# Twelve pairs of a dense expert lookup get their first product early, in a two-block transformer kernel

## The chip, the cores and the metric

The kernel runs on one core of one Trainium2 chip. The metric is the device time of one execution in microseconds; the median of three timed runs is 4170.13 (4164.8 to 4174.73).

## The reference, cut to what matters

Two transformer blocks on 256 tokens of width 1024 in float32. The first block ends in a mixture of 32 experts with two weight matrices in (gate, up) and one out (down), four experts per token. The second block has two streams, context and latent (256 tokens each) and two layers; the context stream goes through the first layer only. Each layer ends in a lookup:

```python
q = (xb @ w_q).reshape(PEER_BLOCK, PEER_HEADS, 2, PEER_HALF)
s = einsum('thpd,pkd->thpk', q, sub_keys)
s1, i1 = top_k(s[:, :, 0], 16)
s2, i2 = top_k(s[:, :, 1], 16)
cand_s = s1[..., :, None] + s2[..., None, :]
cand_i = i1[..., :, None] * 128 + i2[..., None, :]
top_s, pos = top_k(cand_s.reshape(128, 8, 256), 16)
idx = take_along_axis(cand_i.reshape(128, 8, 256), pos)
wts = softmax(top_s)
act = gelu(einsum('thkd,td->thk', u_tab[idx], xb)) * wts
out = einsum('thk,thkd->td', act, v_tab[idx])
```

There are 16384 rows in u_tab and in v_tab. Three such lookups are computed: the context's, the latent's in layer 0, the latent's in layer 1.

## The kernel before, in words

The lookup is computed densely: for all 16384 rows the product with every token, times a grid of gates that is zero where a token did not choose the row. It has two parts.

`peer_prep` (line 808) makes the grid. It multiplies by `w_q` (line 156 to 158), scores the keys (line 723), ranks them on VectorE with `top16` (lines 701 to 709), and reads out the chosen expert numbers (line 760): for each of 8 heads and 16 choices one operation that compares a ramp with the position and sums the candidates' numbers where it matches. That is done for two halves of 128 tokens each. Then `grid` multiplies one-hot matrices (lines 792 to 803) and sends the grid to memory.

`peer_pass` (line 830) goes over 64 pairs of 256 rows each. A pair's first product (`u_stage`, lines 156 to 158, 48 matmuls of 256 columns) needs two weight tiles of 128x1024 from `p_u`. `wload` splits each into a high half (line 146, ScalarE) and a low half (line 147, VectorE), and the product is made of three matmuls, high by high, high by low, low by high. Then come gelu (line 873), the gates (line 894), a split of the result (lines 117, 118), and the second product with two tiles of `p_v` (lines 906 to 909, 24 matmuls of 512 columns), which add up in four PSUM banks over all pairs. Weight tiles rotate over three buffers each of raw, high and low. The latent lookups make 40 and 48 of their pairs' first products ahead of the loop (`early`); those kept in memory are written to `sdr` and read back by `prefetch`.

The experts (`moe`, line 962) run two at a time: gate and up products for two halves of 512 columns (line 1088, each half closed by a bias product, line 1091), a hidden layer, transposes (line 1110), the down product (line 1122) and the sum into tokens (line 1134). Each expert pair needs 24 weight tiles of 1 MB (tile `mo`, four buffers, issued by SyncE).

The order on each engine is made by a scheduler from priorities: the experts come first, and code under `filler` (the context stream and its lookup) fills in. After the first two expert pairs `overflow` (line 1138) tests whether any expert has more than 64 tokens; the test is a branch that every engine takes (line 1143), and the code behind it is issued after it, apart from what the scheduler placed ahead. Of the context lookup's `peer_prep` eight steps are ahead of the test. The last two pairs' loads wait for the last expert load (`late`).

The lines of the change as they are numbered after it stand up to 26 higher: the split is 147 and 148, the test 1155, gate and up 1100, the bias product 1103, down 1134.

Of the kernel before, what the change touches and what calls it, by code (L numbers as in the profile page):

```python
# [10 lines left out]
F32 = mybir.dt.float32  # L11
# [9 lines left out]
P = 128  # L21
# [17 lines left out]
B_LATE = 2  # L39
MT = "u"  # L40
# [4 lines left out]
PF = 2  # L45
# [19 lines left out]
def kernel(ctx: ExitStack, tc: tile.TileContext, a: dict, out: bass.AP):  # L65
# [74 lines left out]
    def wload(src, n=1024, get=load, s=None):  # L140
        wr = wraw(s)
        get(wr[:, :n], src)
        pl, nb = s or (st, WB)
        wh = pl.tile([P, 1024], F32R, tag="wh", name="wh", bufs=nb[1])
        wl = pl.tile([P, 1024], F32R, tag="wl", name="wl", bufs=nb[1])
        nc.scalar.activation(wh[:, :n], wr[:, :n], AF.Copy)  # L146
        low = nc.vector.tensor_sub(wl[:, :n], wr[:, :n], wh[:, :n].bitcast(F32))  # L147
        if hold[1]:
            queued(low, hold[0])
            hold[1] -= 1  # L150
        return wh, wl
# [559 lines left out]
    def topk(l, q, tk, idx, pt):  # L711
        keys, qT = q
        sc = []
        for tb in range(2):
# [42 lines left out]
            for h in range(8):  # L757
                for k in range(16):
                    eq = eqs[:, k % 8, 0:NCAND]
                    nc.vector.scalar_tensor_tensor(eq, iota[:, 0:NCAND], tf[:, h, k:k + 1], ce[:, h, :], op0=ALU.is_equal,  # L760
                                                   op1=ALU.mult, accum_out=ef[:, h, k:k + 1])
                if h % 2:
                    yield
# [66 lines left out]
    def peer_pass(l, xm, pp, gd, consume, ahead=None, after=None, late=None, mark=None, npair=64, wide_end=False):  # L830
# [14 lines left out]
        def fetch(dst, src):  # L845
            ins = nc.sync.dma_start(dst, src)
            queued(ins, after[0] if after else None)
            if late is not None and at_pair[0] >= npair - late[0]:
                queued(ins, late[1])
            if mark is not None:  # L850
                mark[:] = [ins.ins]

        def u_stage(pr, nat):
            bank = psum("u")
            for c in range(2):
# [5 lines left out]
                else:  # L861
                    wh, wl = wload(a["p_u"][l, 2 * pr + c], get=load if pr in rank else fetch)
# [72 lines left out]
        for pr in early:  # L935
# [3 lines left out]
            yield "ahead"  # L939
        grid_fetch(0)  # L940
        prev = None
        for pr in range(npair):
            at_pair[0] = pr
            prefetch(pr + PF)
# [12 lines left out]
        yield npair  # L957

# [263 lines left out]
    with filler():  # L1222
# [31 lines left out]
        bprep = peer_prep(0, XB, tkb, gds[0], (2, NB1, 3), "u")  # L1254
# [4 lines left out]
    with filler():  # L1259
        general("u", "a")  # L1260
        drain(bprep)
        tkb_stack.close()
        pp_stack = ctx.enter_context(ExitStack())
        pp = pool("pp", stack=pp_stack, side="right")
        bpass = peer_pass(0, XB, pp, gds[0], late_res(bres, cdr, 0, 1, 5, pp, "gr"), late=(B_LATE, mres["last"]), mark=bmark)
# [415 lines left out]
```

## Time and profile before

| | us |
|---|---|
| median of three runs | 4170.13 |
| profiled execution | 4162.7 |
| its span | 4160.9 |
| TensorE busy | 4013.7 (96%) |
| VectorE busy | 2382.3 (57%) |
| ScalarE busy | 1929.2 (46%) |
| GpSimd busy | 168.9 (4%) |
| mean granted clock of TensorE | 0.983 |

The page gives the busy time of each engine over the whole span; a view by stages gives it for any stretch, with the granted clock of TensorE and the share of time in which the 16 DMA engines moved data. A timeline gives the start of single instructions and, in brackets, how long the engine sat idle ahead of one and what released it. PE is TensorE, PEld its weight loads, DVE VectorE, ACT ScalarE, POOL GpSimd, SP SyncE; a q behind the name is the engine's sequencer.

### The profile page before, as it was taken

To read this page: it belongs to the slowest core of one execution; us is meant where nothing else is said; L and a number is where in the kernel's file an instruction comes from. 1 tells how busy PE (TensorE), PEld (TensorE's weight loads), DVE (VectorE), ACT (ScalarE), POOL (GpSimd) and SP (SyncE) were. 2 spreads that over 40 slices of the span, in tenths; PEclk is the share of its full clock that TensorE was granted. 3 is DMA by queue.
4 is the path that set the end of the run, shared out by engine and by line. 5 is a ranking of instruction groups with operands and counts; after the bars stand their busy time and mean duration, and the time that the engine had idled before them with its cause. 6 is when DMAs were issued, how large, how long until landed. Compare 5 with 4: busy or idle time off the path is not lost. (4 is left out here: it accounts for less than half of the span.)

```text
span 4160.9 us, 63155 instructions
## 1 busy us (share of the span) xinstructions
PE 4013.7 (96%) x23786; PEld 3064.1 (74%) x23786; DVE 2382.3 (57%) x6357; ACT 1929.2 (46%) x2836; POOL 168.9 (4%) x230
## 2 busy tenths in 40 slices
PE   8999979999999999999998999999998899999998
PEld 7686535566666666666578999788777699988887
DVE  4465686543333333333278997565455789766555
ACT  5543245533333333333243886345545349744443
POOL 0000001100000000000000120000000002200000
PEclk9999989999999999999999999999998899999999
DMA  7659878998889898998865578776774246787773
GB/s 254 240 180 359 338 268 335 348 335 327 338 325 339 322 348 320 338 340 331 319 208 169 205 257 320 258 238 218 261 255 153 98 154 231 260 294 242 235 236 127
DMA packets 340046, 1115.47 MB, mean 268 GB/s; under 512 B 28935, under 2 KB 128007, under 8 KB 283673
## 3 DMA queue, kind: packets, MB, share of 16 engines
q1 hardware_dynamic: 323896, 1043.22, 69.9%
q10 hardware_dynamic: 15552, 66.07, 4.0%
q8 instruction: 189, 3.10, 0.3%
q0 software_dynamic: 288, 2.10, 0.1%
q14 instruction: 121, 0.98, 0.1%
HBM read 1041.97 MB, written 69.30 MB: 267 GB/s over the span
## 5 line engine op out<-in xcount | busy, mean ns | idle before, releaser
L147 DVE TENSOR_TENSOR wl<-wr,wh 128x1024 fp32r<-128x1024 f32 x933 | 1132.1, 1221 | 1045.2 <-ACT wh L146 1038.3
L146 ACT ACTIVATE wh<-wr 128x1024 fp32r<-128x1024 f32 x933 | 980.0, 1055 | 1264.0 <-PE ps_u L157 521.4
L907 PE MATMUL ps_a<-wl,ah 128*128 128x512 f32 x1536 | 587.2, 398 | 2.9 <-DVE wl L147 2.8
L906 PE MATMUL ps_a<-wh,ah 128*128 128x512 f32 x1536 | 572.0, 397 | 0.1
L1088 PE MATMUL ps_g<-mo,xg 128*64 128x512 f32 x2048 | 472.9, 605 | 15.5 <-DMA mo<-in_w_up_dram 11.3
L909 PE MATMUL ps_a<-wh,al 128*128 128x512 f32 x1536 | 478.3, 396 | 0.0
L906 PEld LDWEIGHTS ps_a<-wh,ah 128*128 128x128 f32 x1536 | 288.0, 188 | 79.4 <-issue 12.5
L907 PEld LDWEIGHTS ps_a<-wl,ah 128*128 128x128 f32 x1536 | 286.3, 188 | 76.0 <-issue 13.3
L909 PEld LDWEIGHTS ps_a<-wh,al 128*128 128x128 f32 x1536 | 286.8, 188 | 71.3 <-issue 6.1
L1088 PEld LDWEIGHTS ps_g<-mo,xg 128*64 128x64 f32 x2048 | 137.8, 138 | 269.5 <-issue 236.9
L156 PE MATMUL ps_u<-xbh,wh 128*128 128x256 f32 x1088 | 313.3, 288 | 1.6 <-ACT ge L873 1.6
L157 PE MATMUL ps_u<-xbl,wh 128*128 128x256 f32 x1088 | 312.7, 288 | 0.0
L158 PE MATMUL ps_u<-xbh,wl 128*128 128x256 f32 x1088 | 312.6, 287 | 0.0
L156 PE MATMUL ps_u<-xah,wh 128*128 128x256 f32 x960 | 276.0, 288 | 2.9 <-ACT sp L873 2.7
L158 PE MATMUL ps_u<-xch,wl 128*128 128x256 f32 x960 | 274.1, 287 | 4.1 <-DVE wl L147 4.1
L158 PE MATMUL ps_u<-xah,wl 128*128 128x256 f32 x960 | 273.8, 287 | 2.4 <-DVE wl L147 2.4
L157 PE MATMUL ps_u<-xal,wh 128*128 128x256 f32 x960 | 275.5, 287 | 0.0
L157 PE MATMUL ps_u<-xcl,wh 128*128 128x256 f32 x960 | 274.6, 286 | 0.0
L156 PE MATMUL ps_u<-xch,wh 128*128 128x256 f32 x960 | 274.5, 286 | 0.0
L802 DVE TENSOR_SCALAR o<-cst,it 128x128 f32<-128x128 f32 x768 | 233.2, 347 | 38.8 <-PE ps_a L803 38.3
L1122 PE MATMUL ps_g<-mo,hT 128*64 128x512 f32 x1024 | 239.8, 611 | 8.5 <-DMA mo<-in_w_down_dram 5.3
L803 PE MATMUL ps_a<-o,o 128*128 128x128 f32 x1536 | 227.6, 278 | 11.8 <-ACT o L798 9.4
(652 smaller groups left out, 7004.8 us busy)
## 6 DMA issues: line engine op xcount, KB each, us to landing
wr<-in_p_u_dram SPq DMA_DIRECT2D x384, 512.0 KB, 4.7
wr<-in_p_v_dram SPq DMA_DIRECT2D x384, 512.0 KB, 4.9
mo<-in_w_gate_dram SPq DMA_DIRECT2D x128, 1024.0 KB, 8.5
mo<-in_w_up_dram SPq DMA_DIRECT2D x128, 1024.0 KB, 7.4
mo<-in_w_down_dram SPq DMA_DIRECT2D x128, 1024.0 KB, 8.2
gd<-stg ACTq DMA_DIRECT2D x48, 1024.0 KB, 6.5
gr<-gd SPq DMA_DIRECT2D x96, 512.0 KB, 7.7
mw<-in_w_mod_dram SPq DMA_DIRECT2D x48, 512.0 KB, 5.3
```

Of the source, the lines that this page charges most:

```text
L146: nc.scalar.activation(wh[:, :n], wr[:, :n], AF.Copy)
L147: low = nc.vector.tensor_sub(wl[:, :n], wr[:, :n], wh[:, :n].bitcast(F32))
L156: nc.tensor.matmul(o, wh, xh, start=first, stop=False)
L157: nc.tensor.matmul(o, wh, xl, start=False, stop=False)
L158: nc.tensor.matmul(o, wl, xh, start=False, stop=last)
L802: nc.vector.tensor_scalar(o1, iota, it[:, 0, t:t + 1], it[:, 2, t:t + 1], op0=ALU.is_equal, op1=ALU.mult)
L803: nc.tensor.matmul(bank[:, 2 * i2 + i, :], o2q[:, i, :], o1, start=True, stop=True)
L906: nc.tensor.matmul(acc[tb][hf], ah[:, ts], wh[:, hs], start=first, stop=False)
L907: nc.tensor.matmul(acc[tb][hf], ah[:, ts], wl[:, hs], start=False, stop=False)
L909: nc.tensor.matmul(acc[tb][hf], al[:, ts], wh[:, hf * 512:(hf + 1) * 512], start=False, stop=fin)
L1088: nc.tensor.matmul(bank[64 * i:64 * i + 64, :], xg[:, kq * 4 + k, o:o + CAP], wt[i][:, k, :], start=(kq == 0 and k == 0), stop=False, skip ...
L1122: nc.tensor.matmul(bank[64 * i:64 * i + 64, :], hT[:, kq * 4 + k, 64 * i:64 * i + 64], wt[i][:, k, :], start=(kq == 0 and k == 0), stop=(k ...
```

## The change

Three things change. First, the context lookup's pass is built ahead of its `peer_prep`, and the first products of its pairs 0 to 11 are taken one at a time after every second step of the ranking, so four of them ahead of the overflow test. Their results, after gelu, go to memory and are read back when the loop comes to their pair, into the two buffers of the tile `ge`. Second, the low weight halves of these twelve pairs are subtracted by GpSimd instead of VectorE. Third, in all three lookups the expert numbers are read out for eight heads at once: per choice one compare, one multiplication and one sum over 8x50 elements, in place of eight single steps with a summed output. The scores' banks move from the tag `u` to `a`, and the context's grid uses 4 instead of 6 buffers for its one-hot rows.

```diff
--- before.py
+++ after.py
@@ -37,6 +37,7 @@
 GB = 4
 GG = ('g','u','a','a')
 B_LATE = 2
+N_AHEAD_B = 12
 MT = "u"
 M1, M2, M3 = (2,4,8)
 MI = 14
@@ -137,15 +138,15 @@
     def load(dst, src):
         last_load[0] = nc.sync.dma_start(dst, src).ins
 
-    def wload(src, n=1024, get=load, s=None):
+    def wload(src, n=1024, get=load, s=None, eng=None):
         wr = wraw(s)
         get(wr[:, :n], src)
         pl, nb = s or (st, WB)
         wh = pl.tile([P, 1024], F32R, tag="wh", name="wh", bufs=nb[1])
         wl = pl.tile([P, 1024], F32R, tag="wl", name="wl", bufs=nb[1])
         nc.scalar.activation(wh[:, :n], wr[:, :n], AF.Copy)
-        low = nc.vector.tensor_sub(wl[:, :n], wr[:, :n], wh[:, :n].bitcast(F32))
-        if hold[1]:
+        low = (eng or nc.vector).tensor_sub(wl[:, :n], wr[:, :n], wh[:, :n].bitcast(F32))
+        if hold[1] and eng is None:
             queued(low, hold[0])
             hold[1] -= 1
         return wh, wl
@@ -754,12 +755,13 @@
             nc.vector.tensor_copy(tf, tx)
             ef = tk.tile([P, 8, 16], F32, tag="ef", name="ef")
             eqs = tk.tile([P, 8, 64], F32, tag="sc", name="eq", bufs=2)
-            for h in range(8):
-                for k in range(16):
-                    eq = eqs[:, k % 8, 0:NCAND]
-                    nc.vector.scalar_tensor_tensor(eq, iota[:, 0:NCAND], tf[:, h, k:k + 1], ce[:, h, :], op0=ALU.is_equal,
-                                                   op1=ALU.mult, accum_out=ef[:, h, k:k + 1])
-                if h % 2:
+            eq = eqs[:, :, 0:NCAND]
+            for k in range(16):
+                nc.vector.tensor_tensor(eq, iota[:, None, 0:NCAND].to_broadcast([P, 8, NCAND]), tf[:, :, k:k + 1].to_broadcast([P, 8, NCAND]),
+                                        op=ALU.is_equal)
+                nc.vector.tensor_mul(eq, eq, ce)
+                nc.vector.tensor_reduce(ef[:, :, k:k + 1], eq, axis=AX.X, op=ALU.add)
+                if k % 4 == 3:
                     yield
             ei = tk.tile([P, P], I32, tag="ts", name="ei")
             e2 = tk.tile([P, P], I32, tag="tx", name="e2")
@@ -827,7 +829,7 @@
         drain(first)
         yield from grid(tk, idx[1], gd[1], bufs, 2)
 
-    def peer_pass(l, xm, pp, gd, consume, ahead=None, after=None, late=None, mark=None, npair=64, wide_end=False):
+    def peer_pass(l, xm, pp, gd, consume, ahead=None, after=None, late=None, mark=None, npair=64, wide_end=False, sub_eng=None, pf=PF):
         xh, xl = v3(xm[0]), v3(xm[1])
         acc = []
         n_keep, n_nat, n_ahead, lead, span, ra, rs, xf = ahead or (0, 0, 0, 0, 1, None, None, None)
@@ -846,7 +848,7 @@
             ins = nc.sync.dma_start(dst, src)
             queued(ins, after[0] if after else None)
             if late is not None and at_pair[0] >= npair - late[0]:
-                queued(ins, late[1])
+                queued(ins, late[1]["last"])
             if mark is not None:
                 mark[:] = [ins.ins]
 
@@ -859,7 +861,7 @@
                     for k in range(KD):
                         nc.tensor.matmul(bank[:, c * T:(c + 1) * T], wr[:, k * P:(k + 1) * P], v3(xf)[:, k, :], start=(k == 0), stop=(k == KD - 1))
                 else:
-                    wh, wl = wload(a["p_u"][l, 2 * pr + c], get=load if pr in rank else fetch)
+                    wh, wl = wload(a["p_u"][l, 2 * pr + c], get=load if pr in rank else fetch, eng=sub_eng if pr in rank else None)
                     for k in range(KD):
                         s = slice(k * P, (k + 1) * P)
                         mm3(bank[:, c * T:(c + 1) * T], (wh[:, s], wl[:, s]), (xh[:, k, :], xl[:, k, :]), k == 0, k == KD - 1)
@@ -937,11 +939,13 @@
             if rank[pr] < n_keep:
                 kept[pr] = ge
             yield "ahead"
+        for p in range(pf):
+            prefetch(p)
         grid_fetch(0)
         prev = None
         for pr in range(npair):
             at_pair[0] = pr
-            prefetch(pr + PF)
+            prefetch(pr + pf)
             if pr % 4 == GP:
                 grid_fetch(pr // 4 + 1)
             ge = kept.pop(pr) if pr in rank else u_stage(pr, False)
@@ -955,6 +959,14 @@
             for hf in range(2):
                 consume(tb, hf, acc[tb][hf])
         yield npair
+
+    class Lent:
+        def __init__(self, pl, **bufs):
+            self.pl, self.bufs, self.alias = pl, bufs, {}
+
+        def tile(self, shape, dt, tag, name, bufs):
+            tag = self.alias.get(tag, tag)
+            return self.pl.tile(shape, dt, tag=tag, name=name, bufs=self.bufs.get(tag, bufs))
 
     gds = [[dr.tile([P, 8, P, 16], F32, name=f"gd{i}{b}") for b in range(2)] for i in range(3)]
 
@@ -1251,7 +1263,19 @@
         cx_stack.close()
         tkb_stack = ctx.enter_context(ExitStack())
         tkb = pool("tkb", stack=tkb_stack, side="right")
-        bprep = peer_prep(0, XB, tkb, gds[0], (2, NB1, 3), "u")
+        bpp, bsp = Lent(None), Lent(tkb, sp=1)
+        bpass = peer_pass(0, XB, bpp, gds[0], late_res(bres, cdr, 0, 1, 5, bpp, "gr"), late=(B_LATE, mres), mark=bmark,
+                          ahead=(0, 0, N_AHEAD_B, N_AHEAD_B, 1, None, bsp, None), sub_eng=nc.gpsimd, pf=0)
+        left = [N_AHEAD_B]
+
+        def bsteps():
+            for i, _ in enumerate(peer_prep(0, XB, tkb, gds[0], (2, 4, 3), "a")):
+                if i % 2 and left[0]:
+                    drain(bpass, 1)
+                    left[0] -= 1
+                yield
+
+        bprep = bsteps()
         drain(bprep, PB)
     overflow(mo, mres)
     general("g")
@@ -1259,10 +1283,12 @@
     with filler():
         general("u", "a")
         drain(bprep)
+        drain(bpass, left[0])
         tkb_stack.close()
         pp_stack = ctx.enter_context(ExitStack())
         pp = pool("pp", stack=pp_stack, side="right")
-        bpass = peer_pass(0, XB, pp, gds[0], late_res(bres, cdr, 0, 1, 5, pp, "gr"), late=(B_LATE, mres["last"]), mark=bmark)
+        bpp.pl = bsp.pl = pp
+        bsp.bufs, bsp.alias = {"ge": 2}, {"sp": "ge"}
         drain(bpass)
         general("g")
     acc = mres["acc"]
```

The order of instructions moves as follows. First SyncE, just ahead of the overflow test, before the change; `wr` is a raw weight tile, `mo` an expert's.

```order
L846 DMA wr<-in_p_u_dram 128x1024
L543 DMA mo<-in_w_up_dram 128x2048 x2
L846 DMA wr<-in_p_u_dram 128x1024
L543 DMA mo<-in_w_down_dram 128x2048
L846 DMA wr<-in_p_u_dram 128x1024
L543 DMA mo<-in_w_down_dram 128x2048
L846 DMA wr<-in_p_u_dram 128x1024
L846 DMA wr<-in_p_v_dram 128x1024
L543 DMA mo<-in_w_down_dram 128x2048 x2
L846 DMA wr<-in_p_v_dram 128x1024
L543 DMA mo<-in_w_down_dram 128x2048 x4
L1143 COMPARE_AND_BRANCH
```

And after it, at the same place:

```order
L139 DMA wr<-in_p_u_dram 128x1024
L544 DMA mo<-in_w_down_dram 128x2048
L139 DMA wr<-in_p_u_dram 128x1024
L544 DMA mo<-in_w_down_dram 128x2048
L139 DMA wr<-in_p_u_dram 128x1024
L544 DMA mo<-in_w_down_dram 128x2048
L139 DMA wr<-in_p_u_dram 128x1024
L544 DMA mo<-in_w_down_dram 128x2048 x2
L139 DMA wr<-in_p_u_dram 128x1024 x2
L544 DMA mo<-in_w_down_dram 128x2048 x2
L139 DMA wr<-in_p_u_dram 128x1024 x5
L1155 COMPARE_AND_BRANCH
```

Before, six tiles of the first pairs (two of them of `p_v`) stand ahead of the test, with expert loads last; now thirteen tiles of `p_u` do, five of them last.

Second TensorE at the last expert pair; before, the rows that end its first layer are:

```order
L906 MATMUL ps_a<-wh,ah 128x512
L907 MATMUL ps_a<-wl,ah 128x512
L906 MATMUL ps_a<-wh,ah 128x512
L907 MATMUL ps_a<-wl,ah 128x512
L1088 MATMUL ps_g<-mo,xg 64x512 x8
L1091 MATMUL ps_g<-bgr,sel 128x512
L909 MATMUL ps_a<-wh,al 128x512 x2
L1110 MATMUL ps_g<-cst,hdn 128x128 x4
L1122 MATMUL ps_g<-mo,hT 64x512 x24
L1129 MATMUL ps_g<-cst,og 128x128 x2
```

After, from the down product's end of the last pair but one:

```order
L1100 MATMUL ps_g<-mo,xg 64x512 x16
L1103 MATMUL ps_g<-bgr,sel 128x512
L1100 MATMUL ps_g<-mo,xg 64x512 x16
L1103 MATMUL ps_g<-bgr,sel 128x512
L1100 MATMUL ps_g<-mo,xg 64x512 x16
L1103 MATMUL ps_g<-bgr,sel 128x512
L1100 MATMUL ps_g<-mo,xg 64x512 x8
L1122 MATMUL ps_g<-cst,hdn 128x128 x4
L1100 MATMUL ps_g<-mo,xg 64x512 x8
L1103 MATMUL ps_g<-bgr,sel 128x512
L1122 MATMUL ps_g<-cst,hdn 128x128 x4
L1134 MATMUL ps_g<-mo,hT 64x512 x24
```

Before, products of the lookup (lines 906 to 909, and 156 to 158 further up) stand between the experts' products to the end; now the experts' products stand alone there.

Third GpSimd, after the change, around its branch and at the start of the grid; before, no row of line 147 stood here, and the rest alike.

```order
L1260 DMA cdr<-cz 128x2048
L148 TENSOR_TENSOR wl<-wr,wh 128x1024 x11
L1154 TENSOR_LOAD ci
L1155 COMPARE_AND_BRANCH
...
L148 TENSOR_TENSOR wl<-wr,wh 128x1024 x5
L794 ISA
L794 TENSOR_SCALAR o_8671<-cst,it 128x128 x2
L148 TENSOR_TENSOR wl<-wr,wh 128x1024 x2
L794 TENSOR_SCALAR o_8837<-cst,it 128x128 x2
L148 TENSOR_TENSOR wl<-wr,wh 128x1024
L794 TENSOR_SCALAR o_9000<-cst,it 128x128 x2
L148 TENSOR_TENSOR wl<-wr,wh 128x1024 x2
```

Eleven low halves stand ahead of GpSimd's branch and thirteen behind it, eight of these among the grid's compares (`o`).

## Rows read from the trace of the kernel before

**Rows 1.** Page, part 1: busy us, share of the span, instructions.

```profile
PE 4013.7 (96%) x23786; PEld 3064.1 (74%) x23786; DVE 2382.3 (57%) x6357; ACT 1929.2 (46%) x2836; POOL 168.9 (4%) x230
```

**Rows 2.** Stages: length; busy PE, PEld, DVE, ACT, POOL; clock; DMA share, GB/s.

```profile
495.60:664.20 168.60, 136.50 (x666) 66.80 (x664) 147.31 (x1076) 74.12 (x163) 13.99 (x22) 0.91 0.74 281
664.20:799.50 135.30, 126.15 (x736) 75.58 (x734) 75.57 (x257) 78.14 (x153) 30.47 (x42) 0.99 0.92 351
799.50:1958.40 1158.90, 1154.95 (x6289) 748.19 (x6287) 436.28 (x549) 407.28 (x487) 0.00 (x0) 1.00 0.89 333
1958.40:2090.00 131.60, 126.22 (x650) 73.27 (x649) 41.83 (x51) 36.63 (x44) 0.00 (x0) 0.99 0.83 320
```

**Rows 3.** Slices of 10 us in stage 1, same columns.

```profile
510.00:520.00 10.00, 6.98 (x18) 1.92 (x18) 10.00 (x73) 1.30 (x3) 0.00 (x0) 0.66 0.59 220
520.00:530.00 10.00, 6.69 (x22) 2.04 (x22) 9.96 (x97) 2.36 (x4) 0.00 (x0) 1.00 0.00 1
530.00:540.00 10.00, 3.50 (x10) 2.04 (x11) 9.34 (x77) 0.00 (x0) 0.00 (x0) 0.62 0.20 66
```

**Rows 4.** Line 1143, the overflow test: duration, first and last start us.

```profile
L1143 SPq COMPARE_BRANCH  x1: 50/50/50, 510.5 to 510.5; - x1
L1143 PEldq COMPARE_BRANCH  x1: 3686/3686/3686, 533.2 to 533.2; - x1
L1143 DVEq COMPARE_BRANCH  x1: 76/76/76, 537.1 to 537.1; - x1
```

**Rows 5.** Timeline of PE, starts of first and of second products.

```profile
1958.80 0.28 PE L156 MATMUL ps_u<-xbh,wh 128*128 128x256 f32 x1
1962.64 0.28 PE L158 MATMUL ps_u<-xbh,wl 128*128 128x256 f32 x1
...
987.50 0.39 PE L906 MATMUL ps_a<-wh,ah 128*128 128x512 f32 x1
988.89 0.39 PE L906 MATMUL ps_a<-wh,ah 128*128 128x512 f32 x1
```

**Rows 6.** Lines 147, 792 and 794: ns min/median/max of each.

```profile
L147 DVE TENSOR_TENSOR wl<-wr,wh x933: 426/1226/1249, 9.7 to 4137.3; 128x1024 fp32r<-128x1024 f32 x186, 128x768 fp32r<-128x768 f32 x1
L792 POOL TENSOR_SCALAR o<-cst,it x192: 597/658/1996, 565.1 to 3625.3; 128x128 f32<-128x128 f32 x192
L794 DVE TENSOR_SCALAR o<-cst,it x192: 269/279/398, 706.5 to 3626.5; 128x128 f32<-128x128 f32 x192
```

**Rows 7.** Line 760, the ranking's steps on VectorE.

```profile
L760 DVE SCALAR_TENSOR_TENSOR eq<-cst,tx,ce x768: 218/270/396, 528.1 to 3543.5; 128x50 f32<-128x50 f32 x192
L760 DVE DVE_READ_ACCUMULATOR eq<-cst,tx,ce x768: 72/85/115, 528.3 to 3543.7; 128x1 f32 x192
```

**Rows 8.** Groups by line, VectorE: busy us, mean ns, idle before, releasers.

```profile
L894 DVE TENSOR_TENSOR ge<-ge,gr 128x256 f32<-128x256 f32 x224 | 84.7, 420 | 32.0 <-ACT ge L873 31.9
L118 DVE TENSOR_TENSOR al<-ge,ah 128x512 fp32r<-128x512 f32 x112 | 76.9, 687 | 19.6 <-ACT ah L117 19.4
L894 DVE TENSOR_TENSOR sp<-sp,gr 128x256 f32<-128x256 f32 x120 | 45.3, 422 | 90.1 <-DMA sp<-sdr 40.9 <-DMA gr<-gd 24.5 <-DMA wr<-in_p_v_dram 19.7
```

**Rows 9.** Latent lookups, same columns as rows 2.

```profile
2240.00:2440.00 200.00, 193.49 (x1523) 187.61 (x1522) 191.77 (x1108) 141.85 (x263) 23.05 (x32) 1.00 0.60 204
3340.00:3540.00 200.00, 195.82 (x1522) 188.68 (x1521) 189.70 (x1091) 143.32 (x264) 25.54 (x32) 1.00 0.56 193
```

**Rows 10.** Transfers from 1950 to 2110 us: count, KB each, us to landing.

```profile
mo<-in_w_down_dram SPq DMA_DIRECT2D x14, 1024.0 KB, 4.8
mo<-in_w_gate_dram SPq DMA_DIRECT2D x8, 1024.0 KB
mo<-in_w_up_dram SPq DMA_DIRECT2D x8, 1024.0 KB
```

**Rows 11.** Timeline of PE, the experts' last down products.

```profile
2072.61 3.65 PE L1122 MATMUL ps_g<-mo,hT 128*64 128x512 f32 x16 [1.20 <-DMA mo<-in_w_down_dram]
2078.83 5.24 PE L1122 MATMUL ps_g<-mo,hT 128*64 128x512 f32 x16 [2.56 <-DMA mo<-in_w_down_dram]
```

## The prediction

> **What bounds the kernel now.** I read the page first: TensorE is busy 96% of the span [rows 1], so time can come only from its gaps, its clock, or work moved into them. Next I cut the stretch in which the experts and the context lookup run together at the bias products (line 1091) that end the 4th, 7th, 10th and 30th of the 32 halves of the experts' first layer (495.6, 664.2, 799.5, 1958.4 us), and at the experts' last down product (2090). [...] So stage 3 is TensorE's, stage 2 mostly the DMAs', and stage 1 has room on both.
>
> Stage 1 in slices of 10 us [rows 3]: TensorE 3.5 to 7 us busy while VectorE ranks at 93% to 100%; the DMAs moved 1 GB/s at 520 to 530. The reason stands at the overflow test (line 1143) [rows 4]: SyncE reaches it at 510.5, TensorE at 533.2, VectorE at 537.1, and the next expert weights are issued only after the last of them. Up to there the experts have no weights and the lookup no products.
>
> **The change part by part.** Moved products. A pair's first product is 48 matmuls; they start every 0.12 us (32 of them from 1958.80 to 1962.64) [rows 5]. A pair's second product starts one every 0.232 us (six from 987.50 to 988.89) [rows 5]. Counted in the order of after, 553 more first products stand in stage 1 (all twelve pairs, 576, against 23), 73 fewer in stage 2, 242 fewer in stage 3 and none of the 238 in stage 4; of second products 114 more stand in stage 3, and 6 are left in stage 4 of 118. Nothing is removed from TensorE, so the sum goes by stages.
>
> Stage 1: 136.5 busy + 553 x 0.12 = 66.4 gives 202.9 us. Clock: 9% of 168.6 is 15 us lost now, part of it during idle; with products in the holes I give back 8. Idle left: I take 10 of 32.1, since the gather after the test still waits for VectorE. 204.9 - 168.6 = **+36 us**. Lower end +26 (no idle left), upper end +66 (no hole filled, no clock back). The DMAs have room: 24 loads of 0.52 MB and 12 results of 0.26 MB are 15.7 MB, 41 us at stage 2's 351/0.92 = 381 GB/s, beside 0.74 x 168.6 = 125 busy.
>
> Low halves by GpSimd: 24 of them. No such operation stands in the trace. From below it is VectorE's 1.23 us for this form; from above GpSimd's 658 ns for 128 elements scaled by elements, 5.3 us. The same 128-element compare takes VectorE 279 ns, a ratio of 2.36, which gives 2.9 us [rows 6]; I take that as the nearest row. 24 x 2.9 = 70 us lie on an engine that has 14 us of work in stage 1 [rows 2]. Eleven stand ahead of GpSimd's branch: 32 us from the start of stage 1 (495.6), so they end with TensorE's 533; hidden. SyncE now has 13 weight loads ahead of its branch, the last of which needs the tenth low half, and expert loads stand behind them in its queue. TensorE's own four pairs (23 us, less some 12 of idle filled) bring the test from 537 to about 545; that is within the +36.
>
> Ranking by eight heads: 128 steps of 270 and 85 ns per half lookup [rows 7] are 45.4 us; now 16 times three operations of 400 elements. 256 elements took 420 ns and 512 took 687 [rows 8], so 400 is about 570 ns, 16 x 3 x 0.57 = 27.4 us. VectorE loses 18 us per half, twice per lookup. In the two latent lookups VectorE is busy 191.77 and 189.70 of 200 us but TensorE 193.49 and 195.82 [rows 9]: they have 6.5 and 4.2 us to give. I take **-6** of 10.7; from -11 to +3 (another order of ready work).
>
> Stage 2: 73 products (8.8 us) leave, but the DMAs at 0.92 stay: 0.92 x 135.3 = 124.5 is the floor. **-4** (-11 to 0). Stage 3: 242 x 0.12 = 29 leave, 114 x 0.232 = 26.4 come: -2.6. The twelve results come back from memory one pair ahead only (two buffers), as do the gates; a 256 KB read cost 40.9 us of VectorE waits over the other lookups' 60 [rows 8], about 0.7 each, TensorE has expert work beside it: +3. Together **0** (-5 to +8).
>
> Stage 4 has no pair left to fill it. TensorE: 126.2 - 238 x 0.12 - 112 x 0.232 = 72 us. The experts' 32 loads of 1.05 MB, of which four lie in buffers, are 29.4 MB, and must land one after the other: at 381 GB/s 77 us, at 351 84 us; 30 such loads fall in the stretch now [rows 10]. Where only experts ran at its end, TensorE waited 1.20 and 2.56 us for them [rows 11]. So the DMAs set this stage: 85 us, **-47** (76 to 92 us: -56 to -40).
>
> Sum: 36 - 4 + 0 - 47 - 6 = **-21 us**. What comes after the experts keeps its two held pairs (96 first products) as before. The profiled execution took 4162.7 us (span 4160.9); the median is 4170.13, 7.4 above. 4170.1 - 21 = 4149; I put **4149.0 us**.
>
> [...] VectorE's two-input subtraction [rows 6] took 1226 ns in the median and 1249 at most, GpSimd's compare beside it up to 1996 against 658: if one gave way it was GpSimd, though that compare has a single input. [...]
>
> **The rivals.** (a) The experts' tail is worth less: its chain (hidden layer, transpose, down product) leaves the DMAs at stage 4's present 320 GB/s, 29.4 MB in 92 us, -40, and stage 1 keeps half of its idle, +42. With +4 in stage 3: 42 - 4 + 4 - 40 - 6 = -4, 4166, no change. For it: the order leaves the tail bare, and nothing hides the chain there. Against it: stage 2 reached 351 GB/s beside such chains.
>
> (b) Slower. Place: SyncE's queue ahead of the test. If a low half takes 5.3 us, ten take 53 us from 496 to 549, the pair behind them ends near 560, and expert loads start 23 us later than at 537; fourteen more and the grid's compares then keep GpSimd until about 650, and pairs come every 10.6 us where TensorE needs 5.8. Then no hole is filled: 66 - 4 + 0 - 47 - 6 = +9, 4179. It decides from stage 1's +57 on. VectorE held by GpSimd is the same rival by another way: of the 24 low halves, ten that each stop a two-input step for 2.9 us add 29 us to the engine that sets stage 1, 36 + 29 = +65, +8 in the end. I put .05 of this rival's chance on that way. Against both: GpSimd has few inputs to wait for there, and VectorE's subtraction was never stretched, its ranking step by 126 ns at most [rows 6, 7].
>
> (c) More: stage 1 fills wholly (+26), the tail runs at the best rate (-56) and the latent lookups give all (-11): -45, 4125.
>
> **How the numbers follow.** Forecast .56 (own range 4138 to 4160), (a) .18, (b) .15, (c) .11. 0.2%, about what can be told from no change, is 8.3 us. Faster: .53 of the forecast's .56, .11 of (c) and .03 of (a), .67; same: .03 + .14 + .01 = .18; slower: .14 and .01 of (a), .15. Range: 4122 (c less 3) to 4178 (half of (b)).
>
> **What would show it.** Right: line 148 on GpSimd near 2.9 us; the test passed near 545; the 10th half's bias product some 30 us later than now (799.5), the 30th's too; then pure expert work with TensorE idle on weights, the last down product near 2075; line 760, 762 and 763 near 0.57 us each. Wrong: low halves of 5 us or VectorE steps stretched to 3 us in stage 1, the 10th mark later by over 57 us, or a last stage that still takes over 100 us.

## The result, and the profile after

The changed kernel is slower: 4199.39 us in the median of four runs (4194.81 to 4202.89) against 4169.21 before (4164.8 to 4174.73), a ratio of 1.0084 with a 95% interval from 1.0067 to 1.0101. The profiled span is 4196.3 us, 35.4 more than before. The page's part 1 (busy us, share, instructions):

```profile
PE 4024.4 (96%) x23786; PEld 3068.0 (73%) x23786; DVE 2384.1 (57%) x5085; ACT 1928.9 (46%) x2837; POOL 232.7 (6%) x254
```

Against [rows 1], TensorE runs the same 23786 instructions and is 11 us longer busy with them, VectorE's busy time is within 2 us of what it was, and GpSimd has 64 us more. So some 25 of the 35 us are idle time of TensorE. The stages come next, cut at the same marks as [rows 2] (columns as there): 1 is the ranking of the context lookup, 2 the rest of its grid, 3 the pairs beside the experts, 4 the experts' tail.

```profile
497.20:714.90 217.70, 197.85 (x1235) 133.95 (x1234) 179.28 (x670) 117.32 (x215) 70.17 (x48) 0.97 0.79 296
714.90:858.10 143.20, 122.89 (x645) 67.98 (x643) 69.14 (x245) 71.63 (x140) 25.12 (x38) 0.94 0.88 319
858.10:2014.20 1156.10, 1153.19 (x6161) 739.52 (x6159) 439.17 (x562) 396.58 (x478) 0.00 (x0) 1.00 0.89 334
2014.20:2111.50 97.30, 71.43 (x298) 24.49 (x297) 12.67 (x18) 9.31 (x14) 0.00 (x0) 0.98 0.88 340
```

| term (us, by the traces) | forecast | measured |
|---|---|---|
| stage 1 | +36 | +49 |
| stage 2 | -4 | +8 |
| stage 3 | 0 | -3 |
| stage 4 | -47 | -34 |
| ahead of stage 1 | 0 | +2 |
| latent lookups and what lies between | -6 | +14 |
| sum | -21 | +35 |

TensorE still idles 20 us in stage 1 (32 before), now 20 in stage 2 (9 before) and 26 in stage 4 (5 before). Of the signs of being wrong that the prediction names, one came whole (the 10th mark 58.7 us later, where it says over 57) and one nearly (VectorE's steps stretched to 2.6 us). In stage 4 TensorE waited for expert weights (engine, line, releaser; total us, times, longest), and the second view says what the DMAs moved there:

```profile
PE ps_g L1134 <- DMA mo<-in_w_down_dram: 10.7, 6, 2.6
PE ps_g L1100 <- DMA mo<-in_w_gate_dram: 6.9, 3, 3.2
PE ps_g L1100 <- DMA mo<-in_w_up_dram: 6.0, 4, 2.3
```

```profile
DMA packets 4754, 33.07 MB, mean 340 GB/s; under 512 B 528, under 2 KB 528, under 8 KB 912
```

The overflow test, which stands at line 1155 now, answers to [rows 4]:

```profile
L1155 SPq COMPARE_BRANCH  x1: 50/50/50, 547.6 to 547.6; - x1
...
L1155 DVEq COMPARE_BRANCH  x1: 72/72/72, 553.5 to 553.5; - x1
```

VectorE passes it 16 us later than before, SyncE 37 us later. The low halves (line 148) and the ranking (lines 760, 762, 763), with ns min/median/max, answer to [rows 6, 7]:

```profile
L148 POOL TENSOR_TENSOR wl<-wr,wh x24: 2340/2392/2786, 490.4 to 647.7; 128x1024 fp32r<-128x1024 f32 x24
L760 DVE TENSOR_TENSOR eq<-cst,tx x96: 561/575/2015, 540.2 to 3596.8; 128x400 f32<-128x400 f32 x96
L762 DVE TENSOR_TENSOR eq<-eq,ce x96: 559/575/2622, 540.9 to 3597.4; 128x400 f32<-128x400 f32 x96
L763 DVE TENSOR_REDUCE ef<-eq x96: 555/571/574, 541.5 to 3599.1; 128x8 f32<-128x400 f32 x96
```

The ranking's medians are the forecast ones, and a low half takes 2.39 us where 2.9 were forecast. The greatest values of 760 and 762 are far above their medians; line 763 beside them has no such value. VectorE's timeline in stage 1 (start, us, engine, line, operation):

```profile
526.24 0.28 DVE L710 FIND_INDEX8 x<-m,sc 128x8 uint32<-128x128 f32 x1
526.44 2.22 DVE L741 TENSOR_TENSOR cs<-m 128x64 f32<-128x64 f32 x1
...
530.03 0.43 DVE L702 MAX8 ts<-cs 128x8 f32<-128x50 f32 x3
530.37 2.04 DVE L733 TENSOR_SCALAR x<-x 128x128 f32<-128x128 f32 x1
532.33 0.54 DVE L702 MAX8 ts<-cs 128x8 f32<-128x50 f32 x4
```

and GpSimd's in the same microseconds:

```profile
526.18 2.40 POOL L148 TENSOR_TENSOR wl<-wr,wh 128x1024 fp32r<-128x1024 f32 x1 [4.47 <-ACT wh L147]
529.91 2.42 POOL L148 TENSOR_TENSOR wl<-wr,wh 128x1024 fp32r<-128x1024 f32 x1 [1.33 <-ACT wh L147]
```

An instruction of VectorE that otherwise takes 0.2 us begins under a low half and ends with it (526.18 + 2.40 = 528.58), while searches run through (in stage 1 MAX8 took at most 295 ns, FIND_INDEX8 287). I call this a hold. There are 13 instructions over 1.3 us on VectorE in stage 1, 26.7 us together, some 22 more than such instructions take elsewhere in the trace; before there was none. Next the starts of the ranking's steps: the old ones, in the trace of before,

```profile
546.12 0.27 DVE L760 SCALAR_TENSOR_TENSOR eq<-cst,tx,ce 128x50 f32<-128x50 f32 x1
546.31 0.09 DVE L760 DVE_READ_ACCUMULATOR eq<-cst,tx,ce 128x1 f32 x1
546.31 0.28 DVE L760 SCALAR_TENSOR_TENSOR eq<-cst,tx,ce 128x50 f32<-128x50 f32 x1
```

and the new one:

```profile
557.45 0.57 DVE L760 TENSOR_TENSOR eq<-cst,tx 128x400 f32<-128x400 f32 x1
558.06 0.58 DVE L762 TENSOR_TENSOR eq<-eq,ce 128x400 f32<-128x400 f32 x1
558.67 0.57 DVE L763 TENSOR_REDUCE ef<-eq 128x8 f32<-128x400 f32 x1
```

The old steps start every 0.193 us although the durations of a step and its read add up to 0.36, so 128 of them take 24.7 us. The new chain starts one every 0.609 us, so 48 take 29.2.

### The profile page after: what moved, and what is told of

It is laid out like the page before. It is cut to its first block, busy times and chain, and to the rows that moved or that the text cites. A ratio compares the mean times of both kernels' runs of the same rounds, so it can differ in the third digit from the quotient of the medians.

```text
span 4196.3 us, 61981 instructions
## 1 busy us (share of the span) xinstructions
PE 4024.4 (96%) x23786; PEld 3068.0 (73%) x23786; DVE 2384.1 (57%) x5085; ACT 1928.9 (46%) x2837; POOL 232.7 (6%) x254
## 4 chain that ended last, share of the span: by engine, by line
PE 69%; DVE 8%; DMA 5%; ACT 4%; issue 1%; SPq 0%; POOL 0%; ACTq 0%; DVEq 0%; POOLq 0%
PE ps_g L1100 9%; PE ps_a L909 8%; PE ps_a L908 8%; PE ps_a L911 8%; PE ps_u L157 7%; PE ps_u L159 7%; PE ps_u L158 7%; PE ps_g L1134 4%; PE ps_a L805 2%; DVE wl L148 1%; DMA mo<-in_w_down_dram 1%; ACT wh L147 1%; DVE o L804 1%; PE ps_g L1146 1%; DMA mo<-in_w_up_dram 1%
## 5 line engine op out<-in xcount | busy, mean ns | idle before, releaser
L148 DVE TENSOR_TENSOR wl<-wr,wh 128x1024 fp32r<-128x1024 f32 x909 | 1103.0, 1221 | 932.8 <-ACT wh L147 914.7
L157 PE MATMUL ps_u<-xbh,wh 128*128 128x256 f32 x1024 | 296.2, 289 | 3.3 <-DVEq L1155 3.3
L158 PE MATMUL ps_u<-xbl,wh 128*128 128x256 f32 x1024 | 296.5, 290 | 0.0
L159 PE MATMUL ps_u<-xbh,wl 128*128 128x256 f32 x1024 | 296.4, 289 | 0.0
```

Source lines behind the costliest of these rows:

```text
L148: low = (eng or nc.vector).tensor_sub(wl[:, :n], wr[:, :n], wh[:, :n].bitcast(F32))
L157: nc.tensor.matmul(o, wh, xh, start=first, stop=False)
L158: nc.tensor.matmul(o, wh, xl, start=False, stop=False)
L159: nc.tensor.matmul(o, wl, xh, start=False, stop=last)
```

## The experiments

Ratios are to the kernel before on the same chip, with 95% intervals. "Test" is VectorE's passing of the overflow test and "last product" the end of the experts' last down product (before: 537.1 and 2089.6 us); both are read from one profiled execution, which can lie 7 us from the median. A tag is a set of PSUM banks that tiles take in turn: `u` has two banks and `a` four.

**E1: the new ranking alone,** on the kernel before.

> The kernel before with one part of the change: the expert numbers of all three lookups read out for eight heads at once, no pair moved. Theory T (two causes: the new ranking is longer on VectorE, and the moved pairs put more TensorE work into stage 1 than there is idle): the old steps start every 0.193 us, 128 of them 24.7 us per half lookup; the new chain starts every 0.609 us, 48 of them 29.2 us; so +4.5 us per half, six halves, 27 us of VectorE, of which I expect about 15 to reach the end: 4184 us (4178 to 4191), with line 760's three operations 0.61 us apart here too. Rival R1 (the ranking is neutral, everything comes from the moved pairs): 4169. Rival R2 (the ranking is the whole loss): 4199.

Measured: 4167.47 us, 1.0013 (1.0001 to 1.0024). Test 533.3, last product 2077.6, 12 us earlier than before; from there to the end 13 us longer. So with the new ranking the experts end earlier, which I had not expected, and what comes after them takes longer; the sum is a sixth of the loss. Not all of the 13 us are the new steps': in E5 and E16 below, which keep the old steps there, that stretch is still 7 and 4 us longer than before.

**E2: the move alone,** old ranking put back.

```diff
-            for k in range(16):
-                ...  # compare, multiply, sum for eight heads
+            for h in range(8):
+                ...  # the 128 steps of the kernel before
```

> The changed kernel with the old ranking steps put back; the twelve pairs are moved and GpSimd makes their low halves. T: 4199 less 15 = 4184 us (4177 to 4192); the 10th half's bias product at about 848 us, the last down product near 2102; the latent lookups as long as before. R1 (all from the moved pairs): 4199. R2 (all from the ranking): 4169 or below.

Measured: 4195.02, 1.0077 (1.0062 to 1.0092); test 557.8, last product 2116.4. That is near the rival R1: nearly all of the loss is the move, with what came along.

**E3: low halves on VectorE again.**

```diff
-                          ahead=(...), sub_eng=nc.gpsimd, pf=0)
+                          ahead=(...), sub_eng=None, pf=0)
```

> The changed kernel with the low halves of the twelve pairs on VectorE again. T: GpSimd is no cause; 24 x 1.23 = 29 us more on VectorE in stage 1, which is 179 of 218 us busy there: 4199 to 4220 us, not below 4195. Rival R3 (GpSimd is the cause: SyncE waits 88 us in stage 1 for its low halves, and expert loads stand behind): the test is passed earlier than 550 us and the time falls to 4190 or below.

Measured: 4188.02, 1.0059 (1.0045 to 1.0072), some 10 us better than the changed kernel although VectorE has 27 us of low halves more in stage 1. VectorE is still busy no longer there (177.5 us, 179.3 in the changed kernel): the holds had taken back what the offload saved. My theory of the time fell: GpSimd is a cause. SyncE still waits ahead of the test, here for VectorE's low halves:

```profile
SPq L139 <- DVE wl L148: 20.0, 5, 6.4
```

```profile
L1155 SPq COMPARE_BRANCH  x1: 50/50/50, 543.8 to 543.8; - x1
L1155 DVEq COMPARE_BRANCH  x1: 72/72/72, 546.7 to 546.7; - x1
```

**E4: four pairs,** old ranking (`N_AHEAD_B = 4`, otherwise E2).

> The old ranking steps, the changed kernel's move with 4 pairs in place of 12. T: 4 x 48 x 0.12 = 23 us of products go into stage 1, about 12 of it into idle, so stage 1 is some 11 us longer; the experts' last stage keeps some 31 of its 55 us of lookup work, is still TensorE's and gives all 23 back: 4169 - 12 = 4157 us (4150 to 4168). Rival (the loss of moved pairs is in proportion to their number, as for traffic through memory or waits of the queue): a third of the loss of 12 pairs, 4174.

Measured: 4171.89, 1.0019 (1.001 to 1.0028); test 553.4. That is nearer to the rival: with four pairs, all ahead of the test, the test is nearly as late as with twelve (557.8 in E2).

**E5 and E16: the new ranking in the context lookup alone.**

```diff
+            if pt == "u":
+                ...  # new ranking (context)
+            else:
+                ...  # old steps (latent)
```

> The kernel before with the new ranking in the context lookup alone; the two latent lookups keep the old steps; no pair moved. In the run with the new ranking everywhere the experts' last down product ended 12 us earlier than before and the two latent lookups took about 13 us longer. Theory T2 (the ranking by eight heads helps where the experts run beside it and costs where TensorE has only the lookup): the gain stays and the loss goes, 4163 - 11 = 4152 us (4147 to 4158). Rival (the 12 us are a chance of the order that the latent part gives back anyway): 4163.

> The kernel with the new ranking in the context lookup alone once more, beside the others on one chip: 0.9982 of before, 4156 us; if its gain was chance, 0.9995 or more.

Measured: 4156.27, 0.9982 (0.9973 to 0.9991), and 4156.75, 0.9986 (0.9977 to 0.9995); last product 2076.2 and 2073.4. As expected, this kernel is faster than the one before and than the change; both intervals lie below 1.

**E6: the pairs behind the test,** otherwise E3.

```diff
-                if i % 2 and left[0]:
+                if i >= PB and i % 2 and left[0]:
```

> The changed kernel with the low halves on VectorE (median 4188) and with no moved product ahead of the overflow test: the twelve are taken behind it. T2 (the products ahead of the test push the test, a wait of all engines for one another, from 533 to 547 us, by standing in front of the ranking's own products in TensorE's queue and by weight loads in SyncE's): the test is passed at 533 to 537 again, the 10th half's bias product comes some 10 us earlier, 4188 - 10 = 4178 us. Rival (the moved work costs the same wherever it stands, because stage 1 and the tail are set by sums): 4188.

Measured: 4183.81, 1.0042 (1.0029 to 1.0055); last product 2092.4, 12 us earlier than in E3. The test:

```profile
L1155 SPq COMPARE_BRANCH  x1: 50/50/50, 509.9 to 509.9; - x1
L1155 DVEq COMPARE_BRANCH  x1: 72/72/72, 535.9 to 535.9; - x1
```

The test came where it was expected, and the gain lies between the two theories (4 to 7 us of 10); the times alone do not tell it from none.

**E7: work for GpSimd that nobody reads,** on the kernel before.

```diff
+        left = [56]
+        ...
+                if i % 2 and left[0]:
+                    for _ in range(4):
+                        nc.gpsimd.tensor_sub(junk, XB[0][:, 0:512].bitcast(F32), XB[1][:, 0:512].bitcast(F32))
+                    left[0] -= 4
```

> The kernel before, to which GpSimd does 56 subtractions of 128x512 whose result nobody reads, from the time the context lookup's input is there; the grid's one-hot rows have 4 buffers as in the changed kernel. T2 (while GpSimd subtracts, single VectorE instructions are held until it is done, as 13 instructions of 1.5 to 2.6 us in stage 1 of the changed kernel show, in place of 0.2 to 0.7): VectorE instructions of 0.9 to 1.4 us appear between 499 and 520 us, some 12 us of hold in the sum, the test comes 4 to 8 us later and the time is 4163 + 6 = 4169 us (4164 to 4175). Rival (those long instructions come from something else, as loads of weights, and GpSimd hurts only through SyncE's queue, which nothing here touches): no such instructions, 4163.

Measured: 4199.06, 1.007 (1.0056 to 1.0084). The kernel that differs from it by these subtractions alone is E13 below (1.0038), so they cost about 13 us. VectorE's timeline and GpSimd's beside it (six subtractions in 8.42 us), then the test of E7 and of E13:

```profile
537.25 0.26 DVE L760 SCALAR_TENSOR_TENSOR eq<-cst,tx,ce 128x50 f32<-128x50 f32 x1
...
537.44 1.26 DVE L760 SCALAR_TENSOR_TENSOR eq<-cst,tx,ce 128x50 f32<-128x50 f32 x1
...
538.63 0.26 DVE L760 SCALAR_TENSOR_TENSOR eq<-cst,tx,ce 128x50 f32<-128x50 f32 x1
...
538.82 1.26 DVE L760 SCALAR_TENSOR_TENSOR eq<-cst,tx,ce 128x50 f32<-128x50 f32 x1
```

```profile
535.73 8.42 POOL L1261 TENSOR_TENSOR junk<-xbh,xbl 128x512 f32<-128x512 f32 x6
```

```profile
L1143 SPq COMPARE_BRANCH  x1: 50/50/50, 510.8 to 510.8; - x1
L1143 DVEq COMPARE_BRANCH  x1: 76/76/76, 554.2 to 554.2; - x1
```

```profile
L1143 SPq COMPARE_BRANCH  x1: 50/50/50, 508.4 to 508.4; - x1
L1143 DVEq COMPARE_BRANCH  x1: 76/76/76, 535.2 to 535.2; - x1
```

SyncE is as early as ever, no product is moved, and the test still comes 19 us later: beside the subtractions every second step takes 1.26 us in place of 0.26, and two steps start per subtraction. That is the hold by itself, stronger than I expected.

**E8: fewer loads in the tail,** on the changed kernel; the last expert pair's up products use the gate's weights.

```diff
+                                if e0 == 30 and mi and not moq:
+                                    wt.append(last_gate[i])
+                                    continue
...
+                            last_gate = wt
```

> The changed kernel, but the last expert pair's up products take the gate's weight tiles, so 8 loads of 1.05 MB are left out of the tail; the TensorE work is the same. T2 (the tail without lookup work is set by the expert loads): 8.4 MB at the tail's 341 GB/s are 24.6 us, of which TensorE's 25 us of idle can give some 18: the last stage takes 79 us in place of 97 and the time is 4199 - 18 = 4181 us. Rival (the tail is set by the experts' own chain of first product, hidden layer, transposes and down product): the last stage stays at 97 us, 4199.

Measured: 4185.52, 1.0051 (1.0036 to 1.0065), 14 us less than the changed kernel. The last stage (columns as above):

```profile
2009.80:2097.20 87.40, 71.88 (x296) 24.07 (x294) 13.18 (x18) 9.00 (x13) 0.00 (x0) 0.96 0.72 282
```

It is shorter by 10 us where I expected 18 and the rival none, with TensorE's work unchanged. So the loads do bind this stage, but 15 us of idle stay. Of these, 13.7 are still waits for weights, though the DMAs now move data in 0.72 of the time only; so it is not their rate alone that binds.

**E9 and E14: no pair moved.** E9 is the changed kernel with `N_AHEAD_B = 0`; E14 is the same with 6 buffers for the grid's rows; on every engine its order of instructions is that of E1 with the scores' banks in tag `a`, so the tag is all that sets it apart from E1.

> The changed kernel with no pair moved: the new ranking everywhere, and what came along with the move (4 in place of 6 buffers for the grid's one-hot rows, the scores' banks in another tag, the pass built ahead). Theory T3: these by-works cost nothing, so the time is that of the new ranking alone, 1.0013 of before or 4168 us (4163 to 4174), and the last down product ends near 2077. Rival: the fewer buffers or the shared banks are what the move without GpSimd and behind the test still costs (4184 against 4167): 4180 or more.

> The changed kernel with no pair moved and 6 buffers again. T4: the time of the new ranking alone, 1.0013 of before or 4168 us; stage 2's idle about 6 us. Rival: as with 4 buffers, 1.0048 or 4183 us, stage 2's idle at 15.

Measured: E9 4179.14, 1.0048 (1.003 to 1.0065); E14 4191.07, 1.0073 (1.006 to 1.0085). Both are far above E1, so what came along with the move (the by-works: the tag and the buffers) costs by itself. My theory fell in both, and E14 came out above its rival too. Stage 2 of E1, then of E9:

```profile
656.90:786.50 129.60, 124.04 (x738) 75.52 (x736) 76.07 (x251) 79.34 (x161) 26.70 (x40) 1.00 0.95 349
```

```profile
659.10:790.90 131.80, 116.06 (x639) 66.20 (x637) 69.38 (x241) 75.04 (x157) 25.77 (x40) 0.99 0.89 330
```

TensorE idles there 5.6 us in E1 and 15.7 in E9.

**E13: 4 buffers alone,** on the kernel before.

```diff
-        bprep = peer_prep(0, XB, tkb, gds[0], (2, NB1, 3), "u")
+        bprep = peer_prep(0, XB, tkb, gds[0], (2, 4, 3), "u")
```

> The kernel before with one number changed: the context grid's one-hot rows have 4 buffers in place of 6. Theory T4 (a by-work of the change, the fewer buffers, costs by itself: in every run with 4 buffers TensorE's idle in stage 2 is 14 to 20 us, with 6 it was 5 to 13): stage 2's idle grows from 9 to about 16 us, the last down product comes some 8 us later, 4163 + 8 = 4171 us (4167 to 4177). Rival (the other tag of the scores' banks, or the pass built ahead, is what the run with no pair moved paid for): 4163.

Measured: 4176.05, 1.0038 (1.0025 to 1.0051); stage 2 idles 15.2 us, the grid's last product comes at 844.7 in place of 795.7, the last product at 2098.7. That is what I expected, but E14 shows that 6 buffers under the other tag are worse still: the effects of the two don't add up.

**E10 and E11: four and eight pairs behind the test,** low halves on VectorE, ranking as in E5.

> The new ranking in the context lookup alone, and four pairs moved behind the test with low halves on VectorE. T3 (the twelve pairs cost because they are more than the idle takes and leave the experts' last stage without lookup work, bound by its loads at some 97 us): four pairs are 23 us of products, the last stage keeps about 120 us of TensorE work and stays without idle, so some 8 to 13 us of idle in stages 1 and 2 are won: 4156 - 10 = 4146 us (4140 to 4155). Rival (any product behind the test delays the expert chain more than it fills): 4160 or more.

> As the run before it, with eight pairs. T3: 46 us of products, of which some 20 find idle; the last stage keeps about 100 us of TensorE work against 97 of loads, at the edge: 4150 us (4142 to 4162), between four pairs and what twelve would give with this ranking (4184 - 13 = 4171). Rival: as before, 4165 or more.

Measured: 4182.52, 1.0047 (1.0031 to 1.0063), and 4176.47, 1.0035 (1.0024 to 1.0046). Both missed, and came out where the rival had them (4160 or more, 4165 or more). I had taken E5 as their base, but they carry the by-works that E9 measured. Those are 15 us, and E10 lies 36 us above what I expected; for the rest, the pairs behind the test, with the test no later than before (532.6 and 531.4 us), won nothing that these runs show.

**E12 and E15: two buffers in turn in the ranking,** everywhere (E12) and in the latent lookups alone, the context as in E5 (E15).

```diff
+            for k in range(0, 16, 2):
+                for j in range(2):
+                    nc.vector.tensor_tensor(eq2[j], ...)
+                for j in range(2):
+                    nc.vector.tensor_mul(eq2[j], eq2[j], ce)
+                for j in range(2):
+                    nc.vector.tensor_reduce(..., eq2[j], ...)
```

> The kernel before with the new ranking everywhere, but with two buffers in turn, so that a compare, a multiplication or a sum doesn't follow the one that it needs directly. T3 (the chain of 48 dependent operations costs 0.609 us each because each waits for the one ahead; the old steps overlap): they start about every 0.5 us, 24 us per half in place of 29.2, the latent lookups lose nothing against the old steps, and the gain beside the experts stays: 4167 - 13 = 4154 us (4149 to 4162). Rival (0.57 us is the length of the work itself, and the latent lookups lose by something else): 4167.

> The kernel before with the new ranking as it is in the context lookup, and in the two latent lookups with two buffers in turn. T4: the two-buffer chain is some 1 us per half shorter than the old steps, so the latent lookups give a little: 4156 - 4 = 4152 us (4147 to 4158). Rival (TensorE is the bound there and neither is felt): 4156, as with the old steps.

Measured: E12 4159.88, 0.9991 (0.998 to 1.0001); E15 4148.26, 0.9974 (0.9962 to 0.9985), the lowest time here, though its interval overlaps that of E16. E12 lies inside the range I gave, but not as I thought: the gain beside the experts did not stay (last product 2092.9), and from there to the end it takes 3 us less than before. VectorE's timeline in E15's latent lookup:

```profile
2292.71 0.57 DVE L771 TENSOR_TENSOR eq<-cst,tx 128x400 f32<-128x400 f32 x1
2293.20 1.05 DVE L774 TENSOR_TENSOR eq<-eq,ce 128x400 f32<-128x400 f32 x2
2294.45 1.23 DVE L147 TENSOR_TENSOR wl<-wr,wh 128x1024 fp32r<-128x1024 f32 x1 [0.19 <-ACT wh L146]
2295.59 1.04 DVE L776 TENSOR_REDUCE ef<-eq 128x8 f32<-128x400 f32 x2
```

The multiplication starts 0.49 us after the compare that it doesn't need, not 0.61. A half's reading-out, from first step to last, takes 44.0 us in the first latent lookup, against 52.0 in E1 and 42.4 before.

**E17 and E18: the scores' banks in tag `u` again,** in the changed kernel and in E6.

> The changed kernel, whole, but the scores' banks stay in their old tag, u. Theory T5 (with 6 buffers and no pair moved the only thing left of the change beside the new ranking was the tag, and that kernel took 1.0073 against 1.0013, so the tag a costs some 25 us there: the ranking's scores then share four banks with the grid and the second products): a part of it comes back, 4199 - 12 = 4187 us (4178 to 4195). Rival (the tag only gave another order of ready work, good or bad by chance): 4199 within 6.

> Twelve pairs moved, all behind the test, low halves on VectorE, and the scores' banks in their old tag (that kernel with the new tag: 1.0042, 4184 us). T5: 4184 - 12 = 4172 us (4162 to 4180). Rival: 4184 within 6.

Measured: 4219.99, 1.0145 (1.0127 to 1.0162), and 4190.92, 1.0076 (1.0062 to 1.009). Both theories and both rivals missed: with pairs moved, whose products use the banks `u`, the old tag is worse, by some 25 and 14 us; without them the new tag was, by some 25 (E1 against E14).

## Why the prediction was wrong

The sum had no term for two things that cost most of the loss: the by-works (15 us), and what GpSimd's low halves do to the other engines (10 us). Built up edit by edit, each line is the one above with one thing more:

| kernel | ratio | step, us of 4163 | test | last product |
|---|---|---|---|---|
| new ranking (E1) | 1.0013 | +5 | 533.3 | 2077.6 |
| tag and buffers (E9) | 1.0048 | +15 | 533.6 | 2085.6 |
| twelve pairs, behind the test, low halves on VectorE (E6) | 1.0042 | -2 | 535.9 | 2092.4 |
| four of them ahead of it (E3) | 1.0059 | +7 | 546.7 | 2104.4 |
| low halves on GpSimd (the change) | 1.0084 | +10 | 553.5 | 2111.1 |

Each interval is about 0.0011 to 0.0018 to either side, so a difference of two kernels is known to some 8 or 9 us: the steps of 15 and 10 are clear of that, those of -2 and 7 are not (for the 7, the test and the last product of the two traces lie 11 and 12 us apart).

- **"Hidden"** is the step on the low halves that failed, in two ways. Their duration (2.9 forecast, 2.39 measured) and their place beside an idle engine were right, but they hold VectorE, the last engine to pass the test (553.5 us): 13 holds, 26.7 us in all, in the changed kernel (E3 and E7 show the cost). It was in the text as the second way of rival (b), with a chance of .05 and ten holds of 2.9 us, an estimate: no row of before shows such a hold, and the changed kernel's lasted 2.05 us in the mean. Even so (b) came to +8 only, since it kept the gains of the tail and of the ranking. And they do not stand in a row of 32 us: GpSimd waited 33 us in all for the high halves between the first and the tenth, which ended at 547.2 us, and SyncE passes the test right behind it, at 547.6. How much of E3's 10 us is the hold and how much SyncE's wait, no run separates; E7 shows that a hold can cost as much alone.
- **"Its ranking step by 126 ns at most."** This argument against the hold was right for GpSimd's compare and was carried over to another instruction. In the trace of before the ranking's old steps go on starting every 0.2 us under two compares:

```profile
620.82 1.34 POOL L792 TENSOR_SCALAR o<-cst,it 128x128 f32<-128x128 f32 x2 [7.30 <-PE ps_a L803]
```

```profile
621.51 0.27 DVE L760 SCALAR_TENSOR_TENSOR eq<-cst,tx,ce 128x50 f32<-128x50 f32 x1
...
621.71 0.28 DVE L760 SCALAR_TENSOR_TENSOR eq<-cst,tx,ce 128x50 f32<-128x50 f32 x1
```

Under E7's subtractions the same step took up to 1257 ns, and 9 of the 13 holds in the changed kernel fall on the ranking.
- **The test "to about 545".** It came at 553.5. The products ahead of it moved it by 11 us (E6 to E3: 535.9 to 546.7), where I had put 8; they stand in front of the ranking's own scores in TensorE's queue (the first half's last score comes at 514.9 us, before at 505.4). What the forecast lacked is GpSimd's part, 7 us (E3 to the change): holds, and SyncE's waits for low halves, 40.3 us from the start of stage 1 to its test:

```profile
SPq L139 <- POOL wl L148: 40.3, 8, 11.0
```

- **The by-works had no term.** The buffers and the tag are described ahead of the prediction, and it prices neither; together they cost some 15 us (E9 less E1). In stage 2, put at -4 and measured at +8, TensorE idles 5.6 us in E1, 15.7 in E9 and 20.3 in the changed kernel, so they bear on that too; E6, with the same by-works, idles 11.6 there, and how the rest of it comes about stays open.
- **Ranking: "45.4 us ... 27.4 us".** The old figure added durations that overlap [rows 7]; by starts it was 24.7, so the new one, 29.2, is longer. The stretch after the experts lost 14 us in place of winning 6; E1 and E5, which differ in the latent ranking alone, lie 13 us apart.
- **Stage 1, "I take 10 of 32.1".** TensorE idles 20 us there. The 8 us of clock given back were an estimate; at a clock of 0.97 over 217.7 us some 6.5 are lost where 15 were.
- **Stage 4, "the DMAs set this stage: 85 us".** It took 97. The DMAs do bear on it (E8), and their rate was nearly the forecast one (29.4 MB in 85 us are 346 GB/s, 340 came), but the load was mis-sized: 33.1 MB landed in the stretch, since 30 of the experts' loads were issued in it and not 28, and four of the lookup's of 0.52 MB. At 340 GB/s these are 97 us. With so much less to win in the tail the twelve products behind the test just break even (E6 against E9): TensorE's idle is 21 us less in stages 1 and 2 of E6 and 24 more in stages 3 and 4. Stage 3 came as forecast (-3 for 0).

What stays open: why the buffers and the tag act as they do. 4 buffers cost 16 us under the old tag (E13) and give 10 under the new (E14 to E9), and the tag changes sign with the moved pairs (E14, E17, E18). E1's 12 us gained beside the experts belong here too: the chain got longer there and the experts still came earlier. Each edit gives the scheduler another order of ready work, and orders differed by 10 to 25 us; no run here separates that from the edit itself. So what the by-works cost is measured, and why is not.

## What to carry to other kernels

Price an instruction by the distance of starts, not by its duration (here 0.193 us against 0.36 for the old step), and say whether the next one needs its result (here 0.61 us against 0.49). An engine with nothing to do is not free if its instructions can hold those of the engine that sets the stage (here 13 holds, 26.7 us): ask of each offload whom it can hold, and look for the answer in a row of the same instruction. And price the by-works of a change (two buffers fewer, other banks) with a run in which the change itself does nothing.

## What the runs showed of the hardware

- In the traces here VectorE is held by GpSimd's two-input subtraction until that ends: in stage 1 of the changed kernel each of the 13 held instructions began under a low half and ended 0.07 to 0.43 us after it. There TENSOR_TENSOR took up to 2622 ns and, with one input, TENSOR_SCALAR up to 2280 and CAST up to 2257; MAX8, FIND_INDEX8, MATCH_REPLACE8 and TENSOR_REDUCE stayed within 295, 287, 278 and 574. It was seen the other way as well: the low half that began 0.01 us after a multiplication of VectorE (line 762, 577 ns) took 2786 ns, against 2392 in the median, and E7's subtractions took 1292 ns in the median and up to 2230. GpSimd's compare showed no such hold of VectorE: in the trace of before the ranking's two-input step took at most 396 ns beside it, against 270 in the median [rows 7].
- In the ranking's operations of 128x400 one that doesn't need the operation ahead started about 0.08 us before that one's recorded end (E15: 0.49 us after its start, at 0.57), one that needs it 0.04 us after it (the changed kernel: 0.61).
